# First layer's front: values projected first, POOL work on VectorE, softplus behind the convolution, low parts of weights by half units

## Chip, cores and metric

The kernel runs on one core of a Trainium2 chip. The metric is device time in microseconds (us) of one execution. The engines are TensorE (PE), VectorE (DVE), ScalarE (ACT), GpSimd (POOL) and SyncE (SP), which issues the transfers.

## What is computed

A decoder trunk of two layers over 512 tokens of 1024 features in float32. The change touches the first layer's mixer, and the way in which all weights are prepared:

```
proj = rmsnorm(h) @ w_in                      # 1024 -> y, xr, q, k, v, g of 512 columns each
xr   = causal_depthwise_conv(xr)              # 4 taps over tokens
r, i = sigmoid(block_diag(xr)), sigmoid(block_diag(xr))
a    = exp(-8 r softplus(-lam));  u = sqrt(1 - a^2) * (i * xr)
hs   = scan(a, u)                             # hs[t] = a[t] hs[t-1] + u[t]
lru  = hs * gelu(y)
q, k = rotary(q), rotary(k)                   # cos and sin over 64-wide heads
ret  = groupnorm(retention(q, k, v, decay per head)) * silu(g)
h    = h + concat(lru, ret) @ w_out
h    = h + (silu(hn @ w1) * (hn @ w3)) @ w2   # then sparse attention, and an FFN again
```

## The kernel before, in words

**Products.** The residual lies feature-major on chip, 8 feature tiles (k) of 128 partitions by 512 tokens. Each float32 operand of a large product is split into a high part (rounded to float32r) and a low part (the remainder), and a product is three passes: high by high, high by low, low by high. `hgh` and `hgl` are the parts of the normalised input; `whi` and `wlo` those of a weight unit.

**Weight units.** A unit is 128x2048 (1 MB). `fetch()` loads it (L104), makes its high part on ACT in four pieces of 512 columns (L98) and its low part on DVE in the same four pieces (L99). The pools hold two raw units (`wr`), three high parts (`wh`) and three low parts (`wl`), so that a unit's split can begin only when the unit three places before it is no longer read by PE. A projection uses a pair of units: the first holds feature tiles k = 0 to 3, the second k = 4 to 7.

**Front of layer 0.** The x section (products `ps_x`, L294 to L296) starts while its weights and the input still arrive: per feature tile ACT makes `whi` (L282), `hgh` (L136) and the square `sq` (L148), DVE makes `wlo` (L284) and `hgl` (L137), and POOL adds the squares into `acc` (L150). From `acc` come the RMS factors: `ps_stat` (L160), `ms` (L163), a power on POOL (L165), transposes (L173), `rbc` (L178). `softplus` is some 30 operations on 128x4 elements on DVE and one power on POOL (L239 to L258).

Then come, in program order: the convolution on DVE (`xe` L308, L310, L312) with two gate products per tile (L315) and sigmoids (L316); the projections q, k, v of four token tiles each (`project`, L327; products `ps_t` L123 to L125, 24 a tile); the recurrence (`lru`, L353), whose eight steps are handed out between the tiles of the first projection; `retention_core`; the products `ps_y`, the projection g, and the output projection. A tile of q or k goes through DVE as `e_qk` (L340), through POOL for the cosine product (L343), and through DVE for the sine products `b_qk` (L348, two) and the sums (L350, two). A tile of v leaves PSUM by one ACT operation (L335). In `lru`, POOL makes `u*xc` (L363) and `u*e` (L371); DVE makes three operations per tile (L364 to L366) and the scan (L372).

**Order.** A scheduler of the framework orders the instructions when the program is built, by program order and by the times at which it takes operands to be ready (`fetch` stands a little higher). Each engine then runs its list strictly in that order, and SP issues loads in order too, each when its buffer is free. PSUM has four buffers for `ps_t`, two for gates and transposes.

Of the kernel before, what the change touches and what calls it, by code (L numbers as in the profile page):

```python
"""Two-layer hybrid decoder trunk (RG-LRU + retention, native sparse attention, SwiGLU) on one core.

The residual stays feature-major on chip.  Every float32 operand of a large product is split
exactly into hi + lo parts (hi rounded to float32r, lo the remainder) and the product is the
sum of three float32r passes.  The RMS factor of a token is applied to the products' outputs.
"""
# [8 lines left out]
F32 = mybir.dt.float32  # L15
F32R = mybir.dt.float32r
AF = mybir.ActivationFunctionType
ALU = mybir.AluOpType
# [3 lines left out]
P = 128  # L22
# [22 lines left out]
class Trunk:  # L45
# [43 lines left out]
    def blank(self):  # L89
        """buffers for the next unit: raw, its source, hi, lo"""  # L90
        src, n = self.units.pop(0)
        w = self.wr.tile([P, 2048], F32, tag="wr", name="wr")
        hi = self.wh.tile([P, 2048], F32R, tag="wh", name="whi")
        lo = self.wl.tile([P, 2048], F32R, tag="wl", name="wlo")
        return w[:, 0:n], src, hi, lo

    def split(self, w, hi, lo, c):
        self.nc.scalar.copy(hi[:, c], w[:, c])  # L98
        self.nc.vector.tensor_tensor(lo[:, c], w[:, c], hi[:, c].bitcast(F32), op=ALU.subtract)  # L99

    def fetch(self):
        with self.tc.high_priority(offset=10):
            w, src, hi, lo = self.blank()
            self.nc.sync.dma_start(w, src)  # L104
            n, k = w.shape[1], 4
            for i in range(k):
                self.split(w, hi, lo, slice(i * n // k, (i + 1) * n // k))
        self.ready.append((hi, lo))
# [9 lines left out]
    def mm3(self, ps, terms, first=True, last=True):  # L118
        """ps = sum over terms of (lhs_hi + lhs_lo)^T (rhs_hi + rhs_lo)"""
        mm = self.nc.tensor.matmul  # L120
        n = len(terms)
        for k, (ah, al, bh, bl) in enumerate(terms):
            mm(ps, ah, bh, start=(first and k == 0), stop=False)  # L123
            mm(ps, ah, bl, start=False, stop=False)  # L124
            mm(ps, al, bh, start=False, stop=(last and k == n - 1))  # L125

# [15 lines left out]
    def stat_add(self, k, h, c=slice(0, S), last_apart=False):  # L142
        nc = self.nc
        if k == 0:
            nc.scalar.activation(self.acc[:, c], h, AF.Square)
            return
        sq = self.g2([P, S], name="sq")[:, c]
        nc.scalar.activation(sq, h, AF.Square)  # L148
        if k < KD - 1 or not last_apart:
            nc.gpsimd.tensor_tensor(self.acc[:, c], self.acc[:, c], sq, op=ALU.add)  # L150
        return sq

    def stat_r(self, tiles=range(NT), last=None):
        """1/rms of token tiles as [P, len(tiles)]"""
        nc = self.nc
        n = len(tiles)
        ps = self.psC("ps_stat")
        for j, part in enumerate([self.acc] if last is None else [self.acc, last]):
            for i, t in enumerate(tiles):
                nc.tensor.matmul(ps[:, i:i + 1], part[:, t * P:(t + 1) * P] if j == 0 else part[:, i * P:(i + 1) * P], self.ones[:, 0:1], start=(j == i == 0),  # L160
                                 stop=(i == n - 1 and (j == 1 or last is None)))
        ms = self.s1([P, NT], "ms")[:, 0:n]
        nc.vector.tensor_scalar(ms, ps[:, 0:n], 1.0 / D, EPS, op0=ALU.mult, op1=ALU.add)  # L163
        r = self.const.tile([P, NT], F32, tag="rtok", name="rtok", bufs=2)[:, 0:n]
        nc.gpsimd.tensor_tensor(r, ms, self.mhalf[:, 0:n], op=ALU.pow)  # L165
        return r

    def stat_bc(self, r):
        """1/rms broadcast over partitions, [P, tokens] in PSUM"""
        n = r.shape[1]  # L170
        pb = self.psC("ps_rbc")
        for t in range(n):
            self.nc.tensor.transpose(pb[:, t * P:(t + 1) * P], r[:, t:t + 1].to_broadcast([P, P]), self.ident)  # L173
        return pb[:, 0:n * P]
# [7 lines left out]
    def setup(self):  # L182
        nc, a, c = self.nc, self.a, self.const
        self.vec = c.tile([P, 72], F32, name="vec")
        nc.sync.dma_start(self.vec, a["vec"])
        self.ones = c.tile([P, 8], F32, name="ones")
        nc.vector.memset(self.ones, 1.0)
        # keeps the tensor engine busy until the first operands are there, so that its clock is up by then
        z = self.g2([P, P], name="z")
        nc.vector.memset(z, 0.0)  # L190
        pz = self.psC("ps_z")
        for i in range(10):
            nc.tensor.matmul(pz[:, 0:P], z, z, start=True, stop=True)
        # loads the activation table
        nc.scalar.copy(self.ones[:, 4:8], self.ones[:, 0:4])
        self.mhalf = c.tile([P, 8], F32, name="mhalf")
        nc.vector.memset(self.mhalf, -0.5)
        v = self.vec
        self.gain = [v[:, 8 * i:8 * i + 8] for i in range(5)]
        self.cw = v[:, 40:56].rearrange("p (k m) -> p k m", k=4)  # L200
        self.cb, self.gab, self.gxb, self.lam = (v[:, 56 + 4 * i:60 + 4 * i] for i in range(4))
# [31 lines left out]
    def softplus(self):  # L233
        """4 and -8 times softplus(-lam), [P, 4]"""
# [4 lines left out]
        V.tensor_scalar(z, self.lam, -1.0, None, op0=ALU.mult)  # L239
# [22 lines left out]
    def layer0(self):  # L262
# [22 lines left out]
        for k in range(KD):  # L285
            self.stat_add(k, xin[k // 4][:, k % 4, :])
# [13 lines left out]
        sp4, sp8 = self.softplus()  # L300
# [5 lines left out]
        for m in range(4):  # L306
# [4 lines left out]
            for j in range(1, 4):  # L311
                V.scalar_tensor_tensor(c[:, j:], xe[:, :S - j], self.cw[:, 3 - j, m:m + 1], c[:, j:], op0=ALU.mult, op1=ALU.add)  # L312
            for ax, dst, bias in ((0, tt, self.gab), (1, iv, self.gxb)):
                pg = self.psC("ps_gate")
                T.matmul(pg, self.gw[m // 2][:, m % 2, ax, :], c, start=True, stop=True)  # L315
                last = A.activation(dst[:, m, :], pg, AF.Sigmoid, bias=bias[:, m:m + 1])  # L316
        rdec = {}
# [9 lines left out]
        def project(nm):  # L327
            dst = tok[nm] = self.b8([P, NT, S], name="tok_" + nm)
            w = units()
            for t in range(NT):  # L330
# [7 lines left out]
                else:  # L338
# [4 lines left out]
                    Q.tensor_tensor(d4, e4, self.rcos[:, t:t + 1, :].broadcast_to([P, 2 * RH, 32]), op=ALU.mult)  # L343
# [9 lines left out]
        def lru():  # L353
            # a = exp(-8 sp r) as 1 - w with w = (e + 1) tanh(4 sp r); sqrt(1 - a^2) = sqrt(w (2 - w))
            es = []
            for m in range(4):
# [6 lines left out]
                Q.tensor_tensor(u, u, xc[:, m, :], op=ALU.mult)  # L363
# [4 lines left out]
            for m in range(4):  # L368
                e, t, u = es[m], tt[:, m, :], iv[:, m, :]
                self.after(A.activation(e, e, AF.Sqrt, scale=-1.0), tanh)  # L370
                Q.tensor_tensor(u, u, e, op=ALU.mult)  # L371
# [5 lines left out]
        for nm in "qkv":  # L377
# [43 lines left out]
    def retention_core(self, tok):  # L421
        """normalised retention output of every chunk, token-major; overwrites tok["q"]"""
# [83 lines left out]
    def ffn(self, layer, hg, gain_next, want_hg=True):  # L506
# [50 lines left out]
        # last feature tiles by token halves: the first half is scaled and stored beside the second one's products  # L557
# [18 lines left out]
    def rope(self, x, n, cos, sin):  # L576
        """partial rotary in place on x [P, n, 64] with cos, sin [P, 8]"""
# [11 lines left out]
    def twice(self, dst, src, scale):  # L589
        """dst [P, g, 2, 64] = src [P, g, 64] * scale, in both halves"""  # L590
        self.nc.scalar.activation(dst, src.unsqueeze(2).broadcast_to(list(dst.shape)), AF.Copy, scale=scale)

    def load_gates(self):
        """weights of the branch gates, [hi | lo] side by side as one stationary operand"""
# [9 lines left out]
    def layer1(self, hg):  # L604
# [14 lines left out]
        def pe_bias(x):  # L619
            """the position embedding's product with the first layer's weights, [64, 1]"""  # L620
# [12 lines left out]
        # gates  # L633
        # rows 0..47: hi weights, 48..95: lo
# [64 lines left out]
        def compress():  # L699
            """compressed keys and values: rows (g, n)"""  # L700
# [58 lines left out]
        # queries, rotated; transposed and stacked [hi; lo] (odd heads [lo; hi]) per tile  # L759
# [62 lines left out]
    def attention(self, QS, stack, stacked, qlate, halves, KH, KL, VV, kc2, vc, gate, OH, OL, fill):  # L822
        """softmax attention of the three branches, software-pipelined by hand: in a slot run the scores
        of one head, the scaling of an earlier one and the values of a key block of a still earlier one"""
# [5 lines left out]
        def compressed(i):  # L830
            """scores and weights of the compressed branch for all heads at once: columns (r, g, n)"""
# [206 lines left out]
    def probs(self):  # L1038
        """a [P, 2048] buffer of one of the weight pools"""
# [4 lines left out]
    def final(self, c, last):  # L1044
        """scale and store the tokens of c; last: the squares of the last features"""
# [56 lines left out]
def pack(i):  # L1102
    """inputs laid out as the chip reads them"""
# [19 lines left out]
    # [unit, p, (m, k, c)]  # L1123
    fm = lambda w, mk: c(w.reshape(w.shape[0] // P, P, -1, mk, P).transpose(2, 1, 3, 0, 4).reshape(w.shape[1] // P // mk, P, -1))
    # [unit, p, (k, c)] for column chunks of 512, 4 k-tiles a unit
    tm = lambda w: c(w.reshape(2, 4, P, -1, 512).transpose(3, 0, 2, 1, 4).reshape(-1, P, 2048))
    sec = lambda n: w[:, n * 512:(n + 1) * 512]
    o["w0t"] = tm(np.concatenate([sec(n) for n in (1, 2, 3, 4, 0, 5)], axis=1))
# [33 lines left out]
```

## Time and profile before

| | |
|---|---|
| three runs | 1301.81, 1302.14, 1302.32 us; median 1302.14 |
| span of the profiled execution, first to last instruction | 1299.8 us |
| PE busy in the span | 1272.5 us (98%) |
| DVE / ACT / POOL busy | 708.7 (55%) / 531.7 (41%) / 300.0 (23%) us |

The page gives no time of the profiled execution other than its span; the median of the runs stands 2.3 us above the span, and that is taken for what lies around it. PE's busy time is a modelled one: products are pipelined, each row's length overlaps the next one's, so the distance from start to start is the product's price.

### The profile page before, as it was taken

How to read it: one execution, taken by the hardware profiler on the slowest of the kernel's cores; microseconds unless marked ns; L12 is line 12 of the kernel's file. 1: busy time of each engine (PE TensorE's matmuls, PEld its weight loads, DVE VectorE, ACT ScalarE, POOL GpSimd, SP SyncE). 2: the span in 40 equal slices, each digit the busy share in tenths (PEclk: the TensorE clock that was granted, in tenths of full speed). 3: DMA queues.
4: the chain of work that ended last, by engine and by line, in shares of the span. 5: the costliest groups of instructions: out<-in, count | busy, mean ns of one | idle time of the engine just before them, and what ended most of it. 6: DMA issues, size and time to landing. Idle time of an engine off the chain costs nothing.

```text
span 1299.8 us, 15778 instructions
## 1 busy us (share of the span) xinstructions
PE 1272.5 (98%) x6067; PEld 1049.6 (81%) x6067; DVE 708.7 (55%) x1215; ACT 531.7 (41%) x1121; POOL 300.0 (23%) x304
## 2 busy tenths in 40 slices
PE   8979999999999999999999999999999999999997
PEld 6668888888888888888788877877888888888887
DVE  7994446555423554443345789987345443455433
ACT  6432253433222333334445578996333222233230
POOL 3351421211100111122000467672211100011111
PEclk9999999999999999999999999999999999999999
DMA  6213052222233222252110000024222223322221
GB/s 235 93 65 130 1 185 78 94 97 87 69 120 130 97 97 67 96 198 84 65 65 33 1 1 1 33 66 162 97 98 98 67 89 120 111 95 88 74 71 65
DMA packets 24042, 114.58 MB, mean 88 GB/s; under 512 B 2688, under 2 KB 5008, under 8 KB 14624
## 3 DMA queue, kind: packets, MB, share of 16 engines
q1 hardware_dynamic: 23776, 112.45, 24.9%
q8 instruction: 48, 0.79, 0.2%
q0 software_dynamic: 192, 1.13, 0.2%
q14 instruction: 26, 0.21, 0.0%
HBM read 109.38 MB, written 4.19 MB: 87 GB/s over the span
## 4 chain that ended last, share of the span: by engine, by line
PE 87%; DVE 7%; issue 2%; POOL 2%; ACT 1%; DMA 0%; POOLq 0%; SPq 0%; DVEq 0%; ACTq 0%
PE ps_v L123 6%; PE ps_u L125 6%; PE ps_v L125 6%; PE ps_u L123 6%; PE ps_u L124 6%; PE ps_v L124 6%; PE ps L125 6%; PE ps L123 6%; PE ps L124 6%; PE ps_t L123 4%; PE ps_t L124 4%; PE ps_t L125 4%; PE ps_tr L929 2%; PE ps_s L904 1%; PE ps_p L124 1%
## 5 line engine op out<-in xcount | busy, mean ns | idle before, releaser
L98 ACT CAST whi<-wr 128x512 fp32r<-128x512 f32 (+1 forms) x416 | 212.5, 576 | 394.2 <-PE ps_v L124 162.4
L99 DVE TENSOR_TENSOR wlo<-wr,whi 128x512 fp32r<-128x512 f32 (+1 forms) x416 | 294.4, 763 | 44.3 <-ACT whi L98 44.1
L534 POOL TENSOR_TENSOR v<-v,s 128x512 f32<-128x512 f32 x44 | 67.5, 1535 | 523.2 <-DVE v L533 506.9
L123 PE MATMUL ps<-gh,whi 128*128 128x512 f32 (+1 forms) x374 | 141.0, 377 | 0.0
L124 PE MATMUL ps<-gl,whi 128*128 128x512 f32 (+1 forms) x374 | 140.8, 376 | 0.0
L125 PE MATMUL ps<-gh,wlo 128*128 128x512 f32 (+1 forms) x374 | 140.8, 376 | 0.0
L533 DVE TENSOR_TENSOR v<-ps_v,rbc 128x512 f32<-128x512 f32 x44 | 30.4, 691 | 198.0 <-PE ps_v L125 198.0
L123 PE MATMUL ps_v<-hgh,whi 128*128 128x512 f32 x352 | 137.1, 390 | 0.0
L123 PE MATMUL ps_u<-hgh,whi 128*128 128x512 f32 x352 | 137.1, 390 | 0.0
L125 PE MATMUL ps_u<-hgh,wlo 128*128 128x512 f32 x352 | 137.0, 389 | 0.0
L124 PE MATMUL ps_u<-hgl,whi 128*128 128x512 f32 x352 | 136.9, 389 | 0.0
L124 PE MATMUL ps_v<-hgl,whi 128*128 128x512 f32 x352 | 136.9, 389 | 0.0
L125 PE MATMUL ps_v<-hgh,wlo 128*128 128x512 f32 x352 | 136.9, 389 | 0.0
L124 PE MATMUL ps_t<-wlo,hgh 128*128 128x512 f32 x288 | 113.3, 393 | 6.7 <-DVE wlo L99 6.7
L123 PE MATMUL ps_t<-whi,hgh 128*128 128x512 f32 x288 | 116.0, 403 | 0.0
L125 PE MATMUL ps_t<-whi,hgl 128*128 128x512 f32 x288 | 113.6, 394 | 0.0
L552 DVE TENSOR_TENSOR h<-ps,h 128x512 f32<-128x512 f32 x30 | 20.8, 692 | 135.4 <-PE ps L125 135.4
L924 POOL TENSOR_TENSOR prob<-prob,rs 128x384 f32<-128x384 f32 (+3 forms) x128 | 88.5, 726 | 1.9
L150 POOL TENSOR_TENSOR acc<-acc,sq 128x512 f32<-128x512 f32 (+1 forms) x35 | 48.9, 1398 | 172.1 <-ACT sq L148 171.9
L124 PEld LDWEIGHTS ps<-gl,whi 128*128 128x128 f32 x374 | 70.4, 188 | 13.0
L123 PEld LDWEIGHTS ps<-gh,whi 128*128 128x128 f32 x374 | 70.4, 188 | 12.8
L125 PEld LDWEIGHTS ps<-gh,wlo 128*128 128x128 f32 x374 | 70.4, 188 | 12.8
(282 smaller groups left out, 2291.7 us busy)
## 6 DMA issues: line engine op xcount, KB each, us to landing
wr<-wff SPq DMA_DIRECT2D x44, 1024.0 KB, 4.8
wr<-w SPq DMA_DIRECT2D x32, 704.0 KB, 4.0
wr<-w0t SPq DMA_DIRECT2D x10, 1024.0 KB, 4.8
wr<-w1t SPq DMA_DIRECT2D x10, 1024.0 KB, 4.9
wr<-w0o SPq DMA_DIRECT2D x4, 1024.0 KB, 4.8
wr<-w1o SPq DMA_DIRECT2D x4, 1024.0 KB, 4.9
wr<-w0t SPq DMA_DIRECT2D x8, 256.0 KB, 5.4
xin<-xT SPq DMA_DIRECT2D x8, 256.0 KB, 5.4
```

The lines of the kernel that those rows point to most:

```text
L98: self.nc.scalar.copy(hi[:, c], w[:, c])
L99: self.nc.vector.tensor_tensor(lo[:, c], w[:, c], hi[:, c].bitcast(F32), op=ALU.subtract)
L123: mm(ps, ah, bh, start=(first and k == 0), stop=False)
L124: mm(ps, ah, bl, start=False, stop=False)
L125: mm(ps, al, bh, start=False, stop=(last and k == n - 1))
L150: nc.gpsimd.tensor_tensor(self.acc[:, c], self.acc[:, c], sq, op=ALU.add)
L533: V.tensor_tensor(v, pv, rb, op=ALU.mult)
L534: Q.tensor_tensor(v, v, s, op=ALU.mult)
L552: V.tensor_tensor(hm, ps, hm, op=ALU.add)
L904: T.matmul(u.ps, q, u.kh, start=True, stop=False)
L924: Q.tensor_tensor(x, x, u.rs[:, r, b:b + 1].broadcast_to([P, u.nk]), op=ALU.mult)
L929: T.transpose(u.pt[:, r * P:(r + 1) * P], u.p[:, r, b, j * P:(j + 1) * P], self.ident)
```

## The change

Six edits. (1) The weights' sections are stored in the order x, v, q, k, y, g and the projections run v, q, k; the recurrence's steps now fall between the tiles of v and the first of q. (2) In the front the squares are added on DVE. (3) The cosine products of q and k run on DVE. (4) So do `u*xc` and `u*e` of the recurrence. (5) `softplus` stands behind the convolution and its first operation is held until the last convolution operation. (6) `fetch` still makes four high pieces of 512 columns, and now two low pieces of 1024, each behind two high ones; this holds for all units of the kernel. The rest of the diff takes comments away.

```diff
-            n, k = w.shape[1], 4
-            for i in range(k):
-                self.split(w, hi, lo, slice(i * n // k, (i + 1) * n // k))
+            n = w.shape[1]
+            for i in range(2):
+                for j in range(2 * i, 2 * i + 2):
+                    c = slice(j * n // 4, (j + 1) * n // 4)
+                    self.nc.scalar.copy(hi[:, c], w[:, c])
+                c = slice(i * n // 2, (i + 1) * n // 2)
+                self.nc.vector.tensor_tensor(lo[:, c], w[:, c], hi[:, c].bitcast(F32), op=ALU.subtract)
...
-    def stat_add(self, k, h, c=slice(0, S), last_apart=False):
+    def stat_add(self, k, h, c=slice(0, S), last_apart=False, eng=None):
...
-            nc.gpsimd.tensor_tensor(self.acc[:, c], self.acc[:, c], sq, op=ALU.add)
+            (eng or nc.gpsimd).tensor_tensor(self.acc[:, c], self.acc[:, c], sq, op=ALU.add)
...
-        V.tensor_scalar(z, self.lam, -1.0, None, op0=ALU.mult)
+        self.after(V.tensor_scalar(z, self.lam, -1.0, None, op0=ALU.mult), behind)
...
-            self.stat_add(k, xin[k // 4][:, k % 4, :])
+            self.stat_add(k, xin[k // 4][:, k % 4, :], eng=V)
...
-        sp4, sp8 = self.softplus()
         self.prefetch(2)
...
-                V.scalar_tensor_tensor(c[:, j:], xe[:, :S - j], self.cw[:, 3 - j, m:m + 1], c[:, j:], op0=ALU.mult, op1=ALU.add)
+                last_c = V.scalar_tensor_tensor(c[:, j:], xe[:, :S - j], self.cw[:, 3 - j, m:m + 1], c[:, j:], op0=ALU.mult, op1=ALU.add)
...
+        sp4, sp8 = self.softplus(last_c)
...
-                    Q.tensor_tensor(d4, e4, self.rcos[:, t:t + 1, :].broadcast_to([P, 2 * RH, 32]), op=ALU.mult)
+                    V.tensor_tensor(d4, e4, self.rcos[:, t:t + 1, :].broadcast_to([P, 2 * RH, 32]), op=ALU.mult)
...
-                Q.tensor_tensor(u, u, xc[:, m, :], op=ALU.mult)
+                V.tensor_tensor(u, u, xc[:, m, :], op=ALU.mult)
...
-                Q.tensor_tensor(u, u, e, op=ALU.mult)
+                V.tensor_tensor(u, u, e, op=ALU.mult)
...
-        for nm in "qkv":
+        for nm in "vqk":
...
-    o["w0t"] = tm(np.concatenate([sec(n) for n in (1, 2, 3, 4, 0, 5)], axis=1))
+    o["w0t"] = tm(np.concatenate([sec(n) for n in (1, 4, 2, 3, 0, 5)], axis=1))
```

## Rows read from the trace of the kernel before

**Rows 1.** Stages: us, busy PE PEld DVE ACT POOL, PEclk (granted), DMA share, GB/s

```profile
6.64:34.47 27.83, 25.15 (x104) 19.91 (x105) 24.44 (x50) 16.85 (x32) 10.67 (x8) 0.94 0.72 259
34.47:118.40 83.93, 76.05 (x318) 59.05 (x316) 69.91 (x103) 32.95 (x53) 32.75 (x16) 0.96 0.22 77
118.40:190.00 71.60, 70.68 (x420) 60.44 (x419) 34.30 (x60) 28.31 (x50) 25.02 (x18) 1.00 0.28 100
190.00:1299.80 1109.80, 1096.38 (x5211) 906.15 (x5209) 578.53 (x994) 450.75 (x985) 229.53 (x256) 1.00 0.24 83
```

**Rows 2.** PE's waits over the whole span: total us, times, longest us

```profile
PE ps_t L124 <- DVE wlo L99: 6.7, 1, 6.7
PE ps_x L296 <- DVE hgl L137: 2.7, 2, 1.9
...
PE ps_gate L315 <- DVE xc L312: 0.8, 1, 0.8
```

**Rows 3.** PE's timeline in the front: start us, us, line, tile [idle before <-releaser]

```profile
21.40 0.50 PE L296 MATMUL ps_x<-hgl,whi 128*128 128x512 f32 x1 [1.86 <-DVE hgl L137]
...
25.38 0.39 PE L294 MATMUL ps_x<-hgh,whi 128*128 128x512 f32 x1
...
41.74 3.78 PE L315 MATMUL ps_gate<-xc,gw 128*128 128x512 f32 x8
...
85.83 0.39 PE L123 MATMUL ps_t<-whi,hgh 128*128 128x512 f32 x1
...
89.91 0.39 PE L123 MATMUL ps_t<-whi,hgh 128*128 128x512 f32 x1
97.05 0.79 PE L124 MATMUL ps_t<-wlo,hgh 128*128 128x512 f32 x1 [6.75 <-DVE wlo L99]
```

**Rows 4.** The chain that ended last, 97 to 118 us: start us, us, what

```profile
97.84 0.43 PE ps_t L125
...
100.40 0.27 PE ps_t L125
...
117.49 0.23 PE ps_t L125
```

**Rows 5.** POOL's timeline in the front

```profile
3.28 1.03 POOL L243 TENSOR_TENSOR sp_ex<-sp_base,sp_nz 128x4 f32<-128x4 f32 x1 [1.25 <-DVE sp_nz L241]
...
14.44 1.34 POOL L150 TENSOR_TENSOR acc<-acc,sq 128x512 f32<-128x512 f32 x1 [0.36 <-ACT sq L148]
...
75.67 5.85 POOL L371 TENSOR_TENSOR iv<-iv,e 128x512 f32<-128x512 f32 x4
```

**Rows 6.** DVE's timeline in the front

```profile
12.53 0.17 DVE L245 RECIPROCAL sp_den<-sp_den 128x4 f32<-128x4 f32 x1
...
14.56 1.25 DVE L247 TENSOR_TENSOR sp_s<-sp_s 128x4 f32<-128x4 f32 x1
...
60.19 0.75 DVE L350 TENSOR_TENSOR tok_q<-tok_q,b_qk 128x256 f32<-128x256 f32 x2
...
78.59 3.48 DVE L99 TENSOR_TENSOR wlo<-wr,whi 128x512 fp32r<-128x512 f32 x2
...
96.31 2.49 DVE L99 TENSOR_TENSOR wlo<-wr,whi 128x512 fp32r<-128x512 f32 x4
```

**Rows 7.** ACT's timeline: the high parts of the unit that PE waited for

```profile
84.67 2.18 ACT L98 CAST whi<-wr 128x512 fp32r<-128x512 f32 x4 [11.06 <-PE ps_t L125]
```

**Rows 8.** DVE in 34 to 104 us, chain pieces: the convolution and the scan

```profile
37.95 3.96 DVE xc L312 x6
41.91 1.20 DVE xe L308 x2
43.11 0.91 DVE xc L310 x2
...
82.07 1.13 DVE xc L372
```

**Rows 9.** An FFN unit: its high parts on ACT

```profile
298.18 2.18 ACT L98 CAST whi<-wr 128x512 fp32r<-128x512 f32 x4 [3.90 <-PE ps_v L124]
```

More of the change, by code (lines that the diff above doesn't have):

```diff
@@ L95, in blank @@
         return w[:, 0:n], src, hi, lo
-    def split(self, w, hi, lo, c):
-        self.nc.scalar.copy(hi[:, c], w[:, c])
-        self.nc.vector.tensor_tensor(lo[:, c], w[:, c], hi[:, c].bitcast(F32), op=ALU.subtract)
     def fetch(self):
@@ L231, in setup2, with softplus @@
         self.tneg = tneg
-    def softplus(self):
+    def softplus(self, behind):
         nc = self.nc
```

## Prediction

> **What bounds the kernel now.** I read the stages first [rows 1]: from 118 us on PE is busy at full clock almost without a gap (70.7 of 71.6 us, then 1096 of 1110), so a change to DVE or POOL can give nothing there, only take. In the first 118 us PE is short of work and the granted clock falls to a mean of 0.94 and 0.96, while DVE is busy 24.4 of 27.8 and 69.9 of 83.9 us; v, the last projection of that stage, asks nothing of it, so it must have been about full before. Next, PE's waits [rows 2]: the longest of the kernel, 6.7 us, is for a low part of a weight, the next 2.7 us for `hgl`, both DVE's work. The timelines of PE show what each wait costs beside itself [rows 3, 4]. A product's price at full clock is 0.227 us (85.83 to 89.91, 18 products). After the 1.86 us wait ten products take 25.38 - 21.40 = 3.98 us where 2.27 would do, and after the 6.75 us wait seven take from 97.05 to 100.40, 3.35 us for 1.59. So the two clock losses are 1.7 and 1.8 us.
>
> So the front loses on PE: 2.7 (`hgl`) + 1.7 + 6.75 (low part) + 1.8 = **12.9 us**, and some 0.8 more for the gates, which wait for the convolution. Counted the other way: x, q, k and v are 4 x 96 products, 87.0 us; eight gate products at about 0.8 (the row of 3.78 us holds four, each as two records), RMS sums and transposes add some 7.6; from PE's first product at 6.64 they would end at 101.3. v's last product ends at 117.7 [rows 4]. That is 16.4 us and the upper bound of what a better front can give; the 3.5 us beyond 12.9 are the gates' wait and small lags at changes of work.
>
> Why is DVE late? Its timeline and POOL's side by side [rows 5, 6]. A 128x4 operation takes 0.17 us at 12.53 and 1.25 at 14.56, where POOL's addition runs from 14.44 to 15.78. A pair of low parts, 1.25 us of the four in 2.49, takes 3.48 at 78.59, inside POOL's `u*e` from 75.67 to 81.52. Each POOL operation with inputs in SBUF therefore costs DVE about 1.1 us of standing. And the unit that PE waited for had all of its high parts at 84.67 + 2.18 = 86.85 [rows 7]; its low parts began at 96.31 [rows 6]. For 9.5 us they stood in DVE's list behind the scans and three tiles of k. The list's order did not reckon with the stalls.
>
> **The change part by part.**
>
> *POOL's work on DVE.* In the x section seven additions leave POOL: 7 x 1.1 = 7.7 us of DVE stalls go, 7 x 0.60 come (0.60 is a 512-column low part in [rows 6]: 2.49 for four). In the rest of the front 8 + 4 + 4 POOL operations go: 16 x 1.1 = 17.6 us of stalls. The trace shows no cosine product on DVE. From below it is 0.60; from above it is like two of the 256-column operations on token tiles (0.75 a pair [rows 6]). I take 0.65, since its broadcast operand is the sums' size class: 16 x 0.65 = 10.4 us come. Net, DVE gains 3.5 us in the x section and about 7 behind it; POOL's own 1.3 to 1.5 us latency between `e_qk` and the sums goes too. ScalarE and PE get nothing new.
>
> The Trainium skill, "Perfetto Trace Analysis", § Optimizing Scalar/DVE Operations, says that if DVE is saturated, offloading work to Scalar or even GPSIMD may make sense, though it adds that those two share a port and that it might not help. This change does the opposite in a saturated stretch. By the rule's first half the sum would be 23 more DVE operations, some 15 us, for nothing back; by the 1.1 us of standing it is the net gain above. The rows decide for the page's reservation here.
>
> *Softplus behind the convolution.* In the x section it disappears: 30 operations of at least 0.17 us, and it took the full stalls of POOL's additions. So `hgl`, `wlo` and the addition, each of 512 columns and 0.60 to 0.67, make 1.9 us of DVE per feature tile, against 12 x 0.227 = 2.7 us of PE: PE does not wait there any more, and the 2.7 + 1.7 = 4.4 us come back. Behind the convolution softplus costs DVE 30 x 0.17 = 5.1 us and one power on POOL of 1.03 [rows 5]; what waits for it is only the recurrence's exponentials, whose result is first wanted when `y` is multiplied with it, behind the retention core. It costs nothing as long as v's projection runs over it; without that cover it is 6 us of late low parts.
>
> *Values first.* v's tile needs one ACT operation and no DVE. So for 96 x 0.227 = 21.8 us + 6.4 for gates PE needs from DVE only the convolution and two low parts. From x's new end, 34.5 - 4.4 = 30.1, v ends at about 60, q at 82, k at 104. DVE's ledger from 31: convolution 4 x (0.60 + 0.46 + 3 x 0.66) = 12.2 [rows 8], low parts of the q pair 4.6, softplus 6.1, recurrence 4 x (0.65 + 1.5) + 4 x (0.65 + 1.13) = 15.7: free at about 70, when q's first tile has waited 4 us; PSUM holds four tiles. A q or k tile costs DVE 0.60 + 0.65 + 0.67 + 0.67 = 2.6 us against PE's 5.4; with 4.6 us of low parts per projection DVE has 15 us of work for each 21.8 of PE, and is abreast again in the middle of q to k. What lost its cover is k's last tile: before, v's products ran over its rotation, now the retention core's fourth chunk wants it 2.6 us behind PE's last product of k. The first three chunks and the 96 products of `ps_y` hide it; if the list puts its transposes straight behind k, it costs up to 3 us.
>
> *The low parts' due times.* The second unit of a pair can be split only when PE has read the unit three places back for the last time, which is 24 products, 5.4 us, before its first low part is due. Two high pieces (2 x 0.55) and one DVE operation must fit. A 1024-column piece is not in the trace. By the fixed and the running part of 0.60 for 512 and 0.33 for 256 columns it is 1.14 us (0.06 fixed); from above it is 1.2, two pieces. I take 1.14: it saves 0.12 us a unit on DVE, some 12 us over 104 units, where DVE bounds nothing. The first low part comes later by 0.55 + 0.54 = 1.1 us; of 5.4 us, 3.2 stay for DVE to be late. In the FFN the high parts at 298.18 are released by the unit just finished [rows 9], and two more units of 48 products lie before it, 21.8 us: nothing to pay.
>
> The same section of the Trainium skill's "Perfetto Trace Analysis" says that when Vector isn't saturated but causes bubbles, breaking instructions up may let work be done sooner. That speaks against the half units: by it every pair's second unit would be 1.1 us nearer to a wait. In the trace one such unit was late, by 6.7 us and not by 1; a loss of 1.1 us at each of the ten pairs of both layers' projections would be 11 us, which no other wait on a low part in [rows 2] foreshadows.
>
> *Sum.* From the x section 4.4, from the late low part 6.75 + 1.8 = 8.5; gates unchanged; FFN, attention and end 0. That is 12.9. DVE's ledger is still full between 31 and some 85 us, so I keep back 1.2 us for a low part of the q or k pair that misses its 3.2 us of room (between 0 and, with a clock loss of 1.8, about 9 for two misses of 2.7). **12.9 - 1.2 = 11.7 us**: a span of 1299.8 - 11.7 = 1288.1, with the 2.3 us outside it 1290.4.
>
> **The rivals.**
>
> (a) *A low part is late again, of another pair.* The order is planned anew, DVE is nearly full, and the larger pieces take 1.1 us of the room. For: the ledger above. Against: the 9.5 us of delay came from stalls of 17.6 us that are gone. One or two misses of about 3 us with a clock loss: 4.5 to 9 us back, 1294 to 1299.
>
> (b) *The gain moves on and vanishes.* PE gets ahead of retention, whose chain of chunks takes its own time, and the 12 us turn into waits between chunks. Against: 43.5 us of `ps_y` and g products (2 x 96 x 0.227) are there to fill, and that stage is at 70.7 of 71.6 us [rows 1]. It would give 1301 to 1303.
>
> (c) *Slower: DVE becomes the bound*, if the standing seen in the rows is not POOL's doing, so that the moved work comes on top. DVE's 69.9 us [rows 1] then grow by 10.4 + 6.1 and end, from 31, near 118 instead of 104, with the retention's fourth chunk behind them and no v to hide it. PE fills with `ps_y` while its low parts, queued in the same list, allow. It decides only if DVE runs beyond about 122, when some 5 us of waits with their clock losses stand against the 4.4 us of the x section: 1303 to 1308. The page's advice on a saturated DVE, taken without its reservation, would speak for this one.
>
> **How the numbers follow.** The forecast (11.7, with 9 to 15 as its own range) gets 0.68, (a) 0.22, (b) 0.05, (c) 0.05. Below, the bound is 16.4 us, 1285.7; I put the low end at 1286.5. The high end takes in most of (a): 1298. That leaves out (b), (c) and a little on either side, under 2 in 10. A difference of 0.2%, 2.6 us, is about what a measurement of this kernel can tell from none. Faster by more: the forecast and (a), 0.90; same: (b), 0.05; slower: (c), 0.05.
>
> **What would show it.** In the profile after, the x section has no wait for `hgl`, the clock stays at full through 20 to 30 and 90 to 100 us, `xe` begins some 4 us earlier, a cosine product takes 0.6 to 0.7 us, paired DVE operations of 256 columns go back from 1.8 to 0.75, a low part of 1024 columns takes about 1.2 us, and PE's last product of k ends near 104. The prediction is wrong if a wait of PE on `wlo` of several us stands again in the list of waits, if PE's busy share between 104 and 176 falls, or if waits on low parts appear in the second layer's projections.

## The result, and the profile after

The changed kernel takes 1287.37 us (median of 4 runs, 1287.31 to 1287.63) against 1301.97 before, a ratio of 0.9892, 95% interval [0.9878, 0.9906]: 14.6 us less, where 11.7 were forecast. The span of the profiled execution is 1285.8 us against 1299.8.

The stages of the changed kernel are cut at the start of v's projection (30.00), behind the last of the three projections (104.00) and, as in [rows 1], 1109.8 us before the end (176.00). Each row gives us, then busy PE, PEld, DVE, ACT, POOL, the granted clock, DMA share and GB/s:

```profile
6.64:30.00 23.36, 23.14 (x108) 19.32 (x109) 18.14 (x29) 17.05 (x33) 1.03 (x1) 1.00 0.86 315
30.00:104.00 74.00, 74.00 (x317) 58.02 (x316) 65.28 (x130) 33.36 (x55) 1.39 (x1) 1.00 0.25 86
104.00:176.00 72.00, 71.09 (x421) 60.65 (x420) 36.75 (x58) 27.91 (x49) 23.81 (x18) 1.00 0.29 101
176.00:1285.80 1109.80, 1096.65 (x5208) 905.16 (x5206) 576.50 (x810) 450.48 (x984) 224.97 (x256) 1.00 0.24 83
```

Against [rows 1]: in the first two stages PE is now busy almost from end to end (23.14 of 23.36 us, 74.00 of 74.00), and the granted clock is 1.00, its higher level of 2.4 GHz, where it was 0.94 and 0.96. These two stages together are 14.4 us shorter. The last stage is equally long by the way it is cut; PE's busy time in it is the same within 0.3 us. POOL does one operation in each of the first two stages. Of PE's waits now:

```profile
PE ps_tr L872 <- POOL pcmp L866: 1.2, 1, 1.2
PE ps_x L294 <- ACT hgh L136: 1.1, 1, 1.1
...
PE ps_u L124 <- DVE hgl L137: 0.7, 2, 0.4
```

The waits for `hgl` in x and for `wlo` [rows 2] are gone, those for the gates as well; 0.7 us for `hgl` at the start of the first FFN are new. DVE's timeline in the front is to be held against [rows 6] and [rows 8]:

```profile
30.90 1.29 DVE L307 TENSOR_TENSOR xe<-ps_x,rbc 128x512 f32<-128x512 f32 x2
...
77.28 0.67 DVE L340 TENSOR_TENSOR e_qk<-ps_t,rdec_q 128x512 f32<-128x512 f32 x1
77.99 0.69 DVE L343 TENSOR_TENSOR tok_q<-e_qk,tab 128x512 f32<-128x512 f32 x1
78.60 0.76 DVE L348 TENSOR_TENSOR b_qk<-e_qk,tab 128x256 f32<-128x256 f32 x2
79.27 0.76 DVE L350 TENSOR_TENSOR tok_q<-tok_q,b_qk 128x256 f32<-128x256 f32 x2
...
82.27 2.36 DVE L107 TENSOR_TENSOR wlo<-wr,whi 128x1024 fp32r<-128x1024 f32 x2
```

A tile's rotation runs without a break from 77.28 to 80.0, its cosine product in 0.61 from start to start, and a 1024-column low part takes 1.14 (two in 2.36). And PE at the end of k, with its first product of the output projection:

```profile
102.51 0.39 PE L125 MATMUL ps_t<-whi,hgl 128*128 128x512 f32 x1
102.74 0.60 PE L432 MATMUL ps_tr<-ident,tok_q 128*128 128x128 f32 x4
...
171.88 0.48 PE L123 MATMUL ps_f<-lruH,whi 128*128 128x512 f32 x1
```

The same two products in the kernel before, there at the end of v:

```profile
117.33 0.40 PE L125 MATMUL ps_t<-whi,hgl 128*128 128x512 f32 x1
...
186.64 0.48 PE L123 MATMUL ps_f<-lruH,whi 128*128 128x512 f32 x1
```

The last product of the three projections starts 14.8 us earlier (102.51 instead of 117.33; the 117.7 of [rows 4] is its modelled end), and the output projection is still 14.8 us ahead (171.88 instead of 186.64). The span is 14.0 us shorter, so 0.8 us are given back behind it; the two new waits for `hgl` are 0.7 of them.

### The profile page after: what moved, and what is told of

Read it like the earlier page. It is cut to its first block, busy times and chain, and to the rows that moved or that the text cites. A ratio compares the mean times of both kernels' runs of the same rounds, so it can differ in the third digit from the quotient of the medians.

```text
span 1285.8 us, 15546 instructions
## 1 busy us (share of the span) xinstructions
PE 1269.5 (99%) x6067; PEld 1047.5 (81%) x6067; DVE 697.6 (54%) x1030; ACT 531.5 (41%) x1121; POOL 252.2 (20%) x281
## 4 chain that ended last, share of the span: by engine, by line
PE 93%; DVE 3%; ACT 1%; issue 1%; POOL 1%; DMA 0%; POOLq 0%; SPq 0%; DVEq 0%; ACTq 0%
PE ps_v L123 6%; PE ps_v L125 6%; PE ps_v L124 6%; PE ps L125 6%; PE ps L123 6%; PE ps L124 6%; PE ps_u L124 6%; PE ps_u L125 6%; PE ps_u L123 6%; PE ps_t L123 5%; PE ps_t L125 5%; PE ps_t L124 5%; PE ps_tr L929 2%; PE ps_s L904 1%; PE ps_f L124 1%; PE ps_f L123 1%
## 5 line engine op out<-in xcount | busy, mean ns | idle before, releaser
L107 DVE TENSOR_TENSOR wlo<-wr,whi 128x1024 fp32r<-128x1024 f32 (+1 forms) x208 | 271.2, 1338 | 50.3 <-ACT whi L105 49.2
L531 ACT ACTIVATE s<-s 128x512 f32<-128x512 f32 x44 | 27.8, 633 | 133.0 <-DVE s L530 132.9
```

Of the source, the lines that this page charges most:

```text
L531: A.activation(s, s, AF.Silu)
```

## Experiments

Each is compared with the kernel before, run on the same chip in the same group. Runs 1 to 4, 5 to 8 and 9 to 12 each make a group; the groups' medians of before are 1301.43, 1301.78 and 1300.86 us. Behind a time stand its ratio to before and the 95% interval.

**1. POOL's work back on POOL** (from the changed kernel)

```diff
-            self.stat_add(k, xin[k // 4][:, k % 4, :], eng=V)
+            self.stat_add(k, xin[k // 4][:, k % 4, :])
...
-                    V.tensor_tensor(d4, e4, self.rcos...
+                    Q.tensor_tensor(d4, e4, self.rcos...
...
-                V.tensor_tensor(u, u, xc[:, m, :], op=ALU.mult)
+                Q.tensor_tensor(u, u, xc[:, m, :], op=ALU.mult)
...
-                V.tensor_tensor(u, u, e, op=ALU.mult)
+                Q.tensor_tensor(u, u, e, op=ALU.mult)
```

> The changed kernel with all 23 operations given back to POOL (7 additions of squares, 8 cosine products, 8 products of the recurrence); values first, softplus behind the convolution and half low parts stay. Theory T (POOL's operations make DVE stand, and DVE's standing makes low parts late): the x section stays without waits, since softplus is gone from it (per feature tile 1.27 us of own work + 1.1 of standing = 2.4 against 2.7 of PE), but behind it DVE's ledger grows by 7 us net and a low part is late again: 1291 to 1297 us, with a wait of PE on wlo of 2 to 7 us. Rival C (the order alone does it: v asks nothing of DVE, so its 22 us cover any stall): 1287 to 1289, no wait on wlo.

1299.49 us, ratio 0.9985 [0.9976, 0.9995]: nearly all of the gain is gone, and more than theory T's upper end. One row of PE's waits, and a row each of ACT, DVE and PE, from this run:

```profile
PE ps_t L124 <- DVE wlo L107: 6.2, 3, 3.9
```

```profile
82.32 2.18 ACT L105 CAST whi<-wr 128x512 fp32r<-128x512 f32 x4 [9.27 <-PE ps_t L125]
```

```profile
90.54 2.35 DVE L107 TENSOR_TENSOR wlo<-wr,whi 128x1024 fp32r<-128x1024 f32 x2
```

```profile
91.81 0.50 PE L124 MATMUL ps_t<-wlo,hgh 128*128 128x512 f32 x1 [3.86 <-DVE wlo L107]
```

The picture of [rows 6, 7] is back at the k pair's second unit: high parts done at 84.5, low parts begun 6.0 us later, PE idle for 3.9. In the x section PE has no wait for `hgl`, though the additions are back on POOL: with softplus out of it, the section keeps up.

**2 to 4. The other three edits undone, one at a time** (from the changed kernel)

```diff
-        for nm in "vqk":                      # 2, with the order of the sections
+        for nm in "qkv":
...
+        sp4, sp8 = self.softplus()            # 3, before the convolution
...
-        sp4, sp8 = self.softplus(last_c)
...
+            for j in range(4):                # 4, a high and a low piece of 512 columns each
...
```

> The changed kernel with the projections in the old order q, k, v; POOL's work stays on DVE, softplus behind, half low parts. Theory T: without the standing DVE comes by far less late, 0 to 4 us of waits: 1287 to 1292. Rival C (cover): the wait on a low part in v's projection is back with its clock loss, 8.5 us: 1294 to 1297.

> The changed kernel with softplus before the convolution again. Theory T: its 30 operations no longer meet POOL and cost 0.17 to 0.2 us each; DVE has 1.9 + 0.7 = 2.6 us a feature tile against PE's 2.7, so x waits for 0 to 1.5 us: 1287 to 1289. Rival S (softplus itself held hgl up): the 4.4 us of the x section come back: 1291 to 1293.

> The changed kernel with four low pieces of 512 columns again in every unit. Theory T: low parts are not late anywhere, DVE has room, so nothing: 1287.0 to 1288.0. Rival H (half units are part of the gain, 0.12 us a unit where DVE is full): 1288 to 1291 with a wait on wlo in the front. Rival Q (larger pieces come late somewhere): below 1287.0.

1288.90 (0.9907 [0.9891, 0.9924]), 1288.01 (0.9897 [0.9883, 0.9912]) and 1287.68 us (0.9895 [0.9881, 0.9910]). PE has no wait on `wlo` or `hgl` in the front of any of them; behind it, run 2 has one of 0.6 us for a low part, in the projection g. Each interval holds the changed kernel's ratio: with POOL out of the way, none of these three edits can be told from nothing. The order v, q, k was not needed for the bulk of the gain; rivals C, S, H and Q fall. Run 2's four times, 1288.12 to 1289.73, do all lie above the changed kernel's eight (here and in 12), 1287.23 to 1287.63, so that up to 1.5 us for the order are not excluded.

The profiles show one effect of the half units. The two waits for `hgl` at the start of the first FFN, 0.7 us, stand in every run with half low parts (the changed kernel, 1, 2, 3, 7, 8, 9 and 12) and in none with quarters (before, 4, 5, 6, 10 and 11). It is too small to show in the times.

**5. POOL's work on DVE alone** (from the kernel before: the reverse of 1)

> The kernel before with one edit alone: the 23 POOL operations of the front on DVE. Order q, k, v, softplus in the x section and quarter low parts as before. Theory T: this edit brings nearly all: 1287 to 1290 us, no wait of PE on hgl or on wlo in the front. Rival J (the edits work only together: without v as cover the projections of q and k stay short of low parts): 1292 to 1297.

1287.13 us, ratio 0.9895 [0.9881, 0.9910]: the whole gain, by one of the edits. v's second unit, in the order q, k, v as before, now has its low parts in time; ACT's row and DVE's:

```profile
80.24 2.19 ACT L98 CAST whi<-wr 128x512 fp32r<-128x512 f32 x4 [10.88 <-PE ps_t L125]
```

```profile
82.94 2.49 DVE L99 TENSOR_TENSOR wlo<-wr,whi 128x512 fp32r<-128x512 f32 x4
```

High parts done at 82.4, low parts begun at 82.9: 0.5 us in DVE's list instead of the 9.5 of [rows 6, 7]. Rival J falls.

**6. Values first alone** (from the kernel before)

> The kernel before with the order v, q, k alone; POOL keeps its work. Theory T: the x section keeps its 4.4 us of waits and clock loss, low parts are late again elsewhere: 1299 to 1303. Rival C (cover): 8.5 us of the late low part go: 1292 to 1294.

1293.03 us, ratio 0.9941 [0.9927, 0.9956]. Theory T said too little here and rival C was right: the order by itself removes the late low part (no wait on `wlo` in the front), and the x section keeps a wait for `hgl`:

```profile
PE ps_x L296 <- DVE hgl L137: 1.5, 1, 1.5
```

So there are two cures for the late low part, no standing or more cover, and they do not add up: 8.7 us by the order alone, 14.6 by DVE alone, and no more by both.

**7 and 8. POOL kept busy for nothing** (from the changed kernel; a helper, called beside each of the 23 moved operations; both runs' helpers in one, calls not shown)

```diff
+    def stand(self, x, y):
+        sc = self.g2([P, S], name="stand")
+        self.nc.vector.memset(sc[:, 0:4], 0.0)
+        self.nc.gpsimd.tensor_tensor(sc, x, y, op=ALU.mult)   # 7: reads SBUF
+        for _ in range(2): self.nc.gpsimd.memset(sc, 0.0)     # 8, in its place: writes only
```

> The changed kernel, all its work on DVE, and beside each of the 23 moved operations a POOL product of two 128x512 SBUF inputs whose result nobody uses (and a DVE memset of four columns, 23 x 0.07 = 1.6 us of DVE, that releases it). Nothing waits for the POOL results. Theory T (what costs is POOL reading SBUF beside DVE, not who delivers the result): DVE's two-input operations stand about 1.1 us again beside each, 25 us in all, on top of the moved work, so low parts are late: 1298 to 1308. Rival L (POOL's latency in the chains of the rotation and the recurrence was what cost, and DVE's long operations are something else): 1287 to 1289.

> As the run with the unused POOL products, but each POOL product is two POOL memsets of 128x512, which write SBUF and read nothing; same releasing DVE memsets. Theory T in the form that only POOL's reads stand against DVE's two-input operations: 1287 to 1290, small DVE operations at 0.17 us beside them. Rival B (any POOL instruction blocks DVE, by writing too): several us slower, 1292 to 1303.

1301.01 us (0.9997 [0.9988, 1.0006]) and 1288.48 us (0.9908 [0.9891, 0.9924]). Both have the same instructions on DVE; only POOL's differ. Beside an unused product, a POOL row and a DVE row of run 7:

```profile
87.33 1.52 POOL L143 TENSOR_TENSOR stand<-e_qk 128x512 f32<-128x512 f32 x1 [2.88 <-DVE stand L142]
```

```profile
87.87 1.60 DVE L357 TENSOR_TENSOR b_qk<-e_qk,tab 128x256 f32<-128x256 f32 x2
```

and beside two memsets, the same in run 8:

```profile
79.18 1.11 POOL L144 MEMSET stand<- 128x512 f32 x2 [1.89 <-DVE stand L142]
```

```profile
79.13 0.69 DVE L353 TENSOR_TENSOR tok_q<-e_qk,tab 128x512 f32<-128x512 f32 x1
79.74 0.75 DVE L358 TENSOR_TENSOR b_qk<-e_qk,tab 128x256 f32<-128x256 f32 x2
```

The sine products take 1.60 us under POOL's reading and 0.75 under its writing. In run 7 PE again waits 7.3 us for one low part, though nothing in the kernel needs what POOL makes. Buffers that POOL's reading frees late are not it either: of DVE's waits up to 118 us in run 7, those for POOL are the two that the changed kernel has as well, for the power of the RMS factors (1.1 us, there 1.2) and for softplus's (0.9 in both). Rivals L and B fall: it is POOL's reading of SBUF, not its results being late, that costs. The Trainium skill's "SBUF — State Buffer", § Who interferes with whom, states that a DVE instruction with two SBUF inputs contends with a GpSimd instruction that reads SBUF and not with one that only writes it. The section calls the contention an exclusive lock, with the order of issue deciding who blocks. These two runs agree: in run 7 POOL's row ends at 88.85, and the two sine products end at 89.47, about as much later as two of them take (0.75 in run 8).

**9 and 10. Why undoing edit 1 alone left so little** (from experiment 1)

Before plus values first took 1293.03 (6), but the changed kernel less POOL's move, which is that plus softplus behind and half low parts, 1299.49 (1). So one of those two, or both, cost some 6 us where POOL stays. In 9 softplus goes to the front again, in 10 the low parts are quarters again, with the edits of 3 and 4.

> The changed kernel with all 23 operations back on POOL and softplus before the convolution again; values first and half low parts stay. With POOL's work left alone, values first gave 8.7 us by itself, but together with softplus behind and half low parts only some 2. Theory P (softplus behind the convolution takes v's cover away: its 6 us and the standing of its small operations fill the stretch in which DVE should get ahead): 1292 to 1294. Rival W (the half low parts do it: 1024-column operations stand longer beside POOL and come 1.1 us later): 1298 to 1300.

> The changed kernel with all 23 operations back on POOL and four low pieces of 512 columns again; values first and softplus behind stay. Theory P: nothing changes against the run with POOL's work back, 1298 to 1300, with waits of PE on wlo. Rival W: 1292 to 1294, no such wait.

1294.15 (0.9943 [0.9927, 0.9960]) and 1295.06 us (0.9953 [0.9938, 0.9968]). Neither expectation was right: undoing either one brings most of it back. By the medians each alone costs 1 to 2 us beside values first (up to 3 by the difference to each group's before), and both together 6.5. In 9 the k pair's low parts begin in time, the x section waits for `hgl` 2.7 us again, and one wait of 1.1 us for a low part stands at 159 us, in the projection g. In 10 PE still waits for `wlo`, twice:

```profile
PE ps_t L122 <- DVE wlo L105: 3.7, 2, 3.3
```

against 6.2 us in three waits in run 1. Wait by wait, 1.28 (q), 3.86 (k) and 1.08 us (g, at 164 us) became 0.38, 3.32 and none: each is shorter by 0.5 to 1.1 us, no more than the 1.1 by which a half unit comes later. With the 0.7 us for `hgl` in the FFN, which quarters do not have, that is 3.2 of the 4.4 us between the two runs; the rest was not followed.

**11. The squares alone on DVE** (from the kernel before)

> The kernel before with the seven additions of squares alone on DVE; all other POOL work, the order, softplus and quarter low parts as before. Theory T: the x section's wait for hgl and its clock loss go, 4.4 us, and the late low part of v's second unit stays: 1296.5 to 1298.5. Rival S (softplus, not POOL, holds hgl up): no gain, 1301 to 1303. Rival F (an earlier start of the convolution lets DVE catch up behind it too): below 1294.

1298.47 us, ratio 0.9981 [0.9972, 0.9990]: 2.4 us, less than the 4.4 expected. The wait for `hgl` is gone, and the wait for v's low part stands as it was:

```profile
94.84 0.80 PE L124 MATMUL ps_t<-wlo,hgh 128*128 128x512 f32 x1 [6.69 <-DVE wlo L99]
```

PE goes on 2.2 us earlier than in [rows 3]. The convolution starts at 33.6. Rivals S and F fall. In the profile the missing 2.2 us are the opening: x's first product starts at 7.11 instead of 6.64, and the next ones come some 0.43 us apart for 3.56 us, in which eight products would take 1.8. The profiled execution is the slowest of the ten, though, 1300.22 against a median of 1298.47, so that what the median lacks of 4.4 stays open.

**12. The changed kernel again**

> The changed kernel itself on the chip of this group, as the yardstick for the single edits: 1287 to 1288.5 if the runs of other groups can be compared with it at all.

1287.29 us, ratio 0.9893 [0.9879, 0.9908]. The groups can be compared, and no kernel here beats the changed one clearly; experiment 5 equals it.

## Why the prediction held, and where it was off

*What bounds the front* held. The rows gave the late low part and `hgl`, with their clock losses, as the sum's 12.9 us, and all four terms are gone.

*POOL's work on DVE* held in each number: stalls of 1.1 us per POOL operation vanish, the products cost 0.60 to 0.61 on DVE (0.65 was taken), `xe` starts at 30.9 (31 forecast). Runs 5, 7 and 8 show the cause by itself. The Trainium skill's advice in "Perfetto Trace Analysis", § Optimizing Scalar/DVE Operations, to offload a saturated DVE, which would have spoken for rival (c), is answered by run 1: with the work on POOL, 12 us slower. Its reservation, that GPSIMD and DVE share a port and that moving work between those two might not help, is what these runs bear out.

*Softplus* got credit for the 4.4 us of the x section, and it was one of two cures: PE's wait for `hgl` there is gone with softplus moved and POOL's additions left (1, 10), gone with the additions moved and softplus left (3, 5, 11), and stands only where both are left (before, 6, 9). Runs 1 and 10 have the slow opening of the last section, which gives DVE time: 6, with it, waits 1.5 us where before and 9 wait 2.7. The warning that softplus behind the convolution is 6 us of late low parts without v's cover did not come true: run 2 has neither the cover nor the waits. With POOL's work left, and v first, it did cost: 9 and 1 differ by 5.3 us. *Half low parts* make no difference in the times (4), but "nothing to pay" in the FFN was wrong by the 0.7 us of waits for `hgl`; that the larger pieces bring waits nearer showed there.

*Values first* was given a share that it does not have. The text needed v's cover for DVE to be abreast; run 2 has no such wait without it. The ledger came out somewhat late: q's first tile was taken up at 67.3, the recurrence ended only at 77.3 with that tile and a k unit's low parts done by then, and DVE was abreast, with nothing to do until PE came, only at 95.1, in k and not in the middle of q to k. No low part was late meanwhile, and it would have sufficed in the old order too. k's last tile, uncovered, cost nothing.

*The sum* is the step that was off, by 2.9 us. From the start of PE's first product in x to that of its last in the three projections the time went from 110.7 (6.64 to 117.33) to 95.65 us (6.86 to 102.51): 15.0. Of this 12.9 is the sum's. The other 2.1 are from the 3.5 us that the count by products had shown beyond the named waits. "Gates unchanged" put their part at nothing, but the gates no longer wait (0.8 us in [rows 2]); two operations of the convolution took 3.46 us at 46.51 in the kernel before, beside POOL's row of 5.01 at 44.42, and six take 4.05 at 39.09 now. The rest of the 2.1 was not followed row by row. The reserve of 1.2 us for a missed due time was not needed. Against that, "FFN, attention and end 0" missed the 0.7 us in the FFN. So 15.0, less 0.2 because x begins later and 0.8 behind the output projection's first product, is the span's 14.0, where 11.7 were forecast.

The absolute time has one more error: 2.3 us outside the span came from a median and a span of different executions. Wherever a run has both of the same execution they differ by 1.7 to 2.1 us (1287.63 and 1285.8 in the changed kernel, 1.8), so 1290.4 was about 0.5 us high for this alone. Rivals (a), (b) and (c) did not occur.

## What to carry to other kernels

Before DVE work is spread to POOL, look at DVE's durations while POOL reads SBUF: an operation of 1.3 us on POOL that makes DVE stand for 1.1 costs more than the 0.6 that it takes on DVE itself. A wait of PE on a late operand can be cured by relieving the engine that is late or by covering it with other work. Test each cure alone, for here they did not add up, and an edit that was free with one cost 5 us with the other. When a count of PE's products gives a larger loss than its named waits, part of the remainder may come back as well, as 2.1 of 3.5 us did here.

## Not expected: the opening

Some executions are some 1.7 us later than others before x has well begun. In the changed kernel x's first products come 0.23 us apart; in experiment 6 the first ones come 0.43 apart, and the granted clock by windows of 2 us falls to its lower level, 1.2 GHz (0.50 of full). Its rows, columns here being us, PE busy, clock, DMA share, GB/s:

```profile
4.00:6.00 2.00, 0.94 (x9) 1.00 0.92 307
6.00:8.00 2.00, 1.21 (x4) 0.84 1.02 363
8.00:10.00 2.00, 2.00 (x6) 0.50 0.96 367
10.00:12.00 2.00, 2.00 (x9) 0.81 0.99 377
```

and of the changed kernel:

```profile
6.00:8.00 2.00, 1.15 (x5) 1.00 1.01 365
8.00:10.00 2.00, 2.00 (x11) 1.00 1.06 384
```

Six products instead of eleven in two microseconds show the price. The profiles of 1, 5, 6, 10 and 11 have such an opening; those of before, the changed kernel, 2, 3, 4, 7, 8, 9 and 12 do not. But the granted clock falls only in 1 and 6. In 5, 10 and 11 the products are as far apart under a granted clock of 1.00; the row of 5:

```profile
8.00:10.00 2.00, 2.00 (x7) 1.00 1.05 393
```

The cause stays open. PE had run its warming products and stood idle until the input came, 1.9 us in 6 and 1.1 in the changed kernel, but the length of that idle stretch does not decide: it is 1.1 us in 5 and 0.9 in 10, which have the slow opening, and 1.7 in 2, which has not. That single kernels scatter by 1.5 us (experiment 4: 1286.80 to 1288.28) would fit two kinds of opening, which is not shown. It limits what can be said of edits worth less than 2 us here.
